# Down-projection of a two-layer hybrid block: the low halves and the sums of squares put on VectorE, the last squares given buffers of their own

## The chip, the core and the metric

The kernel runs on one core of a Trainium2 chip. The metric is the time of one execution on the device in microseconds, the median of several. The engines are called by the profile's names: PE (TensorE, matrix products; PEld is its weight loads), DVE (VectorE), ACT (ScalarE), POOL (GpSimd) and SP (SyncE, which issues most of the transfers). Each works through its own queue in order and waits for the others by semaphores.

## The reference

Two layers work on 1024 latent tokens and 256 context tokens of width 1024, all in float32. What matters here is the end of each layer, a squared-ReLU MLP with a hidden width of 4096, and the norm that follows it:

```python
def rmsnorm(x, g):
    xf = x.astype(jnp.float32)
    y = xf * lax.rsqrt(jnp.mean(xf * xf, axis=-1, keepdims=True) + EPS)
    return (y * g.astype(jnp.float32)).astype(x.dtype)

def sqrelu_mlp(h, w_up, w_down):
    return jnp.square(jax.nn.relu(h @ w_up)) @ w_down
...
        x = x + ga2 * sqrelu_mlp(modulate(rmsnorm(x, g_norm2[l]), sh2, sc2), w_up[l], w_down[l])
        if not last:
            ...
            xc = xc + ga2c * sqrelu_mlp(modulate(rmsnorm(xc, g_norm2[l]), sh2c, sc2c), w_up[l], w_down[l])
    return rmsnorm(x, g_final)
```

The change touches the product with `w_down`, the residual add behind it, and the sum of squares for the next norm.

## The kernel before

Activations lie transposed: features on the 128 partitions, tokens along the row. Block 0 and block 1 are 512 latent tokens each, block 2 is the context (only in layer 0, where the flag `ctx_all` is set). `xT[b]` holds eight tiles of block b's residual stream and `ss[b]` its running sum of squares.

**Products in three passes.** A product must be more exact than one pass of PE. Every operand is therefore split: the high half is a rounded copy made on ACT (L147), the low half is the difference of the operand and that copy (L148), on DVE or POOL. `mm3` then takes high times high (L134), high times low (L135) and low times high (L136).

**Which engine makes a low half** is set by a letter pattern. `lo_(pat)` counts its calls and returns POOL where the pattern has a G and DVE where it has a V. The down-projection's pattern is `DL`, used by `cAt` and `cBt`, which split the two operands of a product into the eight buffers of the tile `A1` (the activations' `cA`, the weights' `cB`; in layer 0 a ninth in a tile `c`). The combinations' pattern `DA` is all V.

**The down-projection** sums over the hidden width in four chunks. A chunk takes a 2 by 2 grid of blocks by Strassen's scheme: seven calls of `run`, each four steps of twelve matmuls, on ready blocks or on sums and differences of blocks that `comb` makes in place (L1445, two instructions of 128x1024 on DVE for each). The blocks lie in `r2`, `A0` and `wr` tiles. In layer 0 each chunk also does the context rows in one pass (`ctx_part`, L1466).

**The residual add** is `put` (L1420, DVE): it multiplies a result in PSUM, or a copy of it in SBUF, by the gate and adds it to `xT[b]`. In the last chunk each `put` of a tile also squares the tile on ACT into a scratch buffer `sc` (L1425) and adds it to `ss[b]` (L1426); the first square of a block goes into `ss[b]` directly (L1423). `psl` is a list of spare half tiles; `sc` is its entries 8 to 11 (two halves of a `c` tile, then `p` or `wf` tiles).

**The norm behind it.** `rstd_bcast` sums `ss[b]` over the partitions by PE (L194), takes the inverse root by three Newton steps of tiny instructions on DVE (L175 to L187) and spreads it over the partitions by PE (L201). After layer 0, `raw` (L1190, L1192) makes the next layer's input of it. After layer 1, `finish_(0)` copies the factor of block 0 into `sc[1]` (L1481), multiplies five tiles by it on POOL (L1487) and three on DVE (L1489), and stores them. Block 1 ends in two halves of 256 tokens: `put`-like adds (L1576), squares (L1577), sums (L1578), two norms, and outputs on POOL (L1587) and DVE (L1590).

**Order.** The program is written as one stream; a scheduler with its own estimates of durations sets each engine's order. A change of engines therefore also moves neighbours.

Of the kernel before, what the change touches and what calls it, by code (L numbers as in the profile page):

```python
# [9 lines left out]
ALU = mybir.AluOpType  # L10
# [24 lines left out]
FA = "V"  # L35
LF = "V"
DA = "V"
DL = "VVVG"
RQ = "MAAV"
NQ = (3, 8)  # L40
GU = 7
SE = ((1, 1), (1, 0))
GL = 100
TQ = 1
LNE = (0, 1)
# [18 lines left out]
def build(tc, A, out, dbg=None):  # L64
# [9 lines left out]
    def T(pool, shape, dt=F32, tag=None, **kw):  # L74
        if tag in alias:
            tag, kw = alias[tag], {}
            if isinstance(tag, tuple):
                pool, tag = tag
        assert kw == seen.setdefault((id(pool), tag), kw) or not kw, tag
        kw = seen[(id(pool), tag)]  # L80
        return pool.tile(list(shape), dt, tag=tag, name=nm(tag), **kw)
# [24 lines left out]
    V, S, G, PE = nc.vector, nc.scalar, nc.gpsimd, nc.tensor  # L106
# [211 lines left out]
    ss = [T(xp, [128, BLK[b][1]], tag=f"ss{b}") for b in range(3)]  # L318
# [109 lines left out]
    for l in range(2):  # L428
        last = l == 1
# [172 lines left out]
        sc = V.tensor_tensor_scan  # L602
# [439 lines left out]
        xT, ss, yT, wo = [None] * 3, [None] * 3, [None] * 3, []  # L1042
# [190 lines left out]
        def csplit(src, pat, c=None):  # L1233
            c = ctile() if c is None else c
            split((c[:, 0], c[:, 1]), src, lo=lo_(pat))
            return c
# [16 lines left out]
        def P_(tag="p"):  # L1253
            return T(*((wk, [128, 512]) if tag == "p" else (ring, [128, 512])), tag=tag)
# [141 lines left out]
        psl = [t[:, i] for t in ct for i in range(2)] + [P_() for _ in range(3 if ctx_all else 9)]  # L1396
        if ctx_all:
            psl += [P_("wf") for _ in range(3)]
        u2, u3, sc = psl[0:4], psl[4:8], psl[8:12]
        nc_ = [0, 0]  # L1400

        def cAt(src):
            nc_[0] += 1
            return csplit(src, DL, cA[nc_[0] % len(cA)])

        def cBt(src):
            nc_[1] += 1
            return csplit(src, DL, cB[nc_[1] % len(cB)])

# [5 lines left out]
        def gains(b, j):  # L1415
            return modT[l][:, BLK[b][2], 40 + j:41 + j]

        def put(b, j, src, sq=None, eng=None):
            xj = xT[b][:, j]
            V.scalar_tensor_tensor(xj, src, gains(b, j), xj, ALU.mult, ALU.add)  # L1420
            if sq is not None:
                if nss[b] == 0:
                    S.activation(ss[b], xj, AF.Square)  # L1423
                else:
                    S.activation(sq, xj, AF.Square)  # L1425
                    (eng or G).tensor_tensor(ss[b], ss[b], sq, ALU.add)  # L1426
                nss[b] += 1

        wdn = A["w_dn"][l].rearrange("(p h) q t -> p h q t", h=2)
        NCH = NPR // 4  # L1430
        E0, E1 = [(G, V)[i] for i in SE[l]]
        blk = {}
# [23 lines left out]
        def ctx_part(c, lastc):  # L1456
            f = A2t[:, c % 2]
            for i in range(2):
                nc.sync.dma_start(f[:, 2 * i:2 * i + 2], dac[4 * c + 2 * i:4 * c + 2 * i + 2].rearrange("p q t -> q p t"))
            ps = banks("Y")  # L1460
            for q in range(2):
                for jj in range(4):
                    o = ps[2 * q + jj // 2][:, 256 * (jj % 2):256 * (jj % 2) + 256]
                    for h in range(2):
                        for k in range(4):
                            PE.matmul(o, blk[f"B{h + 1}{q + 1}"][k][:, 128 * jj:128 * jj + 128], f[:, k, 256 * h:256 * h + 256],  # L1466
                                      start=h + k == 0, stop=h * k == 3)
                    put(2, 4 * q + jj, o, sc[jj][:, :256] if lastc else None)
# [27 lines left out]
        for c in range(NCH):  # L1496
            lastc = c == NCH - 1
# [13 lines left out]
            for j in range(4):  # L1511
                put(0, j, X[j])
# [4 lines left out]
            for j in range(4):  # L1517
                put(0, j, Y[j], sc[j] if lastc else None)
# [38 lines left out]
            for j in range(4):  # L1557
                S.copy(u3[j], X[j])
            for j in range(4):
                put(1, 4 + j, u3[j], sc[j] if lastc else None, E1)  # L1560
            if not lastc:
                p3()
            if lastc and last:
# [5 lines left out]
                for th in range(2):  # L1569
# [4 lines left out]
                    for j in range(4):  # L1574
                        xj, sq = xT[1][:, j, tl], u2[j][:, tl]
# [107 lines left out]
def make(A, dbg=None):  # L1683
    import concourse.bacc as _bacc
    nc = _bacc.Bacc("TRN2", target_bir_lowering=False, num_devices=1)
    aps = {}
    for name, a in A.items():
        aps[name] = nc.dram_tensor(f"in_{name}", a.shape, mybir.dt.from_np(a.dtype), kind="ExternalInput").ap()
    o = nc.dram_tensor("out_0", (128, 8, 1024), F32, kind="ExternalOutput").ap()
    with tile.TileContext(nc, schedule_with_timeline_sim=True) as tc:  # L1690
        build(tc, aps, o, dbg)
    return nc
# [9 lines left out]
```

## Time and profile before

| quantity | value |
|---|---|
| median of 3 runs | 3015.47 us (3014.15 to 3018.77) |
| profiled execution | 3019.14 us, of which the span of the trace is 3017.3 us |
| down-projection of layer 0, with the norm behind it | about 1238 to 1690 us |
| down-projection of layer 1, to the end | about 2661 to 3017 us |
| mean granted clock of PE | 0.962 |

How to read it: the profile names an instruction by line, engine and tiles (output, then inputs, without buffer numbers). A group's row gives its count, its busy time, the mean duration, the idle time of the engine before its members and what ended most of that. A row of the timeline gives the start, the duration, and in brackets the idle time ahead of it and what ended it. The table of stages gives for each stretch the busy time of each engine, then the clock that PE was granted (1.00 is full speed).

### The profile page before, as it was taken

The numbers are of one execution on the slowest core, as the hardware profiler recorded it, in microseconds if no ns is written. First come the engines' busy times: TensorE is split into PE (matmuls) and PEld (weight loads), VectorE is DVE, ScalarE is ACT, GpSimd is POOL, SyncE is SP. The second block draws the span as 40 slices with busy tenths as digits, with TensorE's granted clock in tenths as the row PEclk, the third lists the DMA queues.
The fourth block names the chain that finished last, engine by engine and source line by source line (L and its number), as shares of the span: only waits on it lengthen the run. The fifth ranks groups of instructions, "written<-read, shape, count | busy, mean of one in ns | idle before, by whom it ended". The sixth has DMA issues, their size and how long they took to land.

```text
span 3017.3 us, 40556 instructions
## 1 busy us (share of the span) xinstructions
PE 2827.9 (94%) x14320; PEld 2334.7 (77%) x14320; DVE 2128.6 (71%) x4170; ACT 1178.6 (39%) x2283; POOL 517.3 (17%) x517
## 2 busy tenths in 40 slices
PE   7988989989989999999999898899999999989996
PEld 6877867757878888888887787867767788868885
DVE  8769668742498898786787527468633976678887
ACT  3322245443353333243245432245433534334444
POOL 4213100011200000021125133100022000013334
PEclk7999999999999999999999999899999999999998
DMA  6514575323355544633121212455134443253321
GB/s 237 161 55 128 146 174 156 110 91 120 109 175 175 168 171 165 240 112 116 45 91 56 88 42 85 124 147 147 56 120 139 146 134 115 105 198 99 105 85 56
DMA packets 277871, 376.44 MB, mean 125 GB/s; under 512 B 63396, under 2 KB 154468, under 8 KB 276004
## 3 DMA queue, kind: packets, MB, share of 16 engines
q1 hardware_dynamic: 274788, 366.51, 39.0%
q0 software_dynamic: 576, 4.20, 0.4%
q10 hardware_dynamic: 2304, 3.15, 0.3%
q8 instruction: 113, 1.85, 0.3%
q14 instruction: 90, 0.74, 0.1%
HBM read 283.74 MB, written 90.02 MB: 124 GB/s over the span
## 4 chain that ended last, share of the span: by engine, by line
PE 59%; DVE 18%; DMA 10%; issue 6%; POOL 2%; ACT 2%; SPq 0%; DVEq 0%; POOLq 0%; ACTq 0%
PE mm L138 9%; PE mm L143 7%; PE mm L144 7%; PE v L1141 4%; PE mm L135 4%; PE mm L136 4%; PE mm L134 4%; DVE junk L235 3%; DVE A L148 2%; DVE ac L677 2%; PE mm L1466 2%; PE mm L140 2%; PE mm L141 2%; DMA wf<-in_w_mt 2%; PE t L1466 2%
## 5 line engine op out<-in xcount | busy, mean ns | idle before, releaser
L138 PE MATMUL mm<-A,wr 128*128 128x512 f32 (+1 forms) x840 | 312.9, 375 | 24.6 <-ACT rb L673 12.3
L135 PE MATMUL mm<-A 128*128 128x512 f32 (+1 forms) x654 | 251.3, 389 | 11.2 <-DVE A L148 8.9
L134 PE MATMUL mm<-A 128*128 128x512 f32 (+1 forms) x654 | 238.1, 387 | 5.6 <-ACT A L147 4.4
L136 PE MATMUL mm<-A 128*128 128x512 f32 (+1 forms) x654 | 242.9, 387 | 0.3 <-DVE A L148 0.3
L138 PEld LDWEIGHTS mm<-A,wr 128*128 128x128 f32 x840 | 161.2, 193 | 54.0 <-ACT rb L673 14.0
L143 PE MATMUL mm<-A,wr 128*128 128x512 f32 (+1 forms) x520 | 193.0, 372 | 6.2 <-DVE A L148 4.2
L144 PE MATMUL mm<-A,wr 128*128 128x512 f32 (+1 forms) x520 | 191.6, 369 | 0.0
L1141 PE MATMUL v<-PT,Vt 128*97 128x512 f32 (+1 forms) x336 | 172.8, 599 | 16.6 <-ACT PT L1140 16.1
L138 PE MATMUL mm<-A,c 128*128 128x512 f32 (+1 forms) x520 | 184.0, 355 | 4.5 <-ACT A L147 3.4
L143 PE MATMUL mm<-A,c 128*128 128x512 f32 (+1 forms) x520 | 184.3, 355 | 2.7 <-DVE A L148 2.6
L144 PE MATMUL mm<-A,c 128*128 128x512 f32 (+1 forms) x520 | 182.5, 353 | 1.3 <-DVE c L148 1.3
L148 POOL TENSOR_TENSOR wr<-wf,wr 128x512 fp32r<-128x512 f32 x88 | 123.7, 1413 | 292.1 <-ACT wr L147 230.3
L147 ACT ACTIVATE A<-wr 128x512 fp32r<-128x512 f32 x188 | 114.2, 625 | 147.9 <-PE mm L135 59.2
L147 ACT ACTIVATE A<-A 128x512 fp32r<-128x512 f32 x174 | 106.9, 625 | 160.0 <-PE mm L135 86.6
L148 DVE TENSOR_TENSOR A<-wr,A 128x512 fp32r<-128x512 f32 x146 | 128.7, 893 | 43.4 <-ACT A L147 29.0
L235 DVE SCALAR_TENSOR_TENSOR junk<-wf,t 128x512 bf16<-128x512 f32 x192 | 130.8, 681 | 33.7 <-DMA wf<-in_w_mt 32.0
L135 PEld LDWEIGHTS mm<-A 128*128 128x128 f32 x654 | 123.9, 190 | 39.4 <-DVE A L148 11.7
L1140 ACT ACTIVATE PT<-s 128x512 f32<-128x512 f32 (+1 forms) x168 | 97.0, 583 | 138.6 <-PE s L144 138.0
L134 PEld LDWEIGHTS mm<-A 128*128 128x128 f32 x654 | 123.1, 189 | 31.2 <-ACT A L147 6.8
L136 PEld LDWEIGHTS mm<-A 128*128 128x128 f32 x654 | 123.5, 189 | 25.0 <-DVE A L148 0.7
L138 PE MATMUL mm<-wr,A 128*128 128x256 f32 x464 | 133.4, 288 | 6.6 <-ACT rb L673 4.7
L143 PE MATMUL mm<-wr,A 128*128 128x256 f32 x464 | 133.1, 288 | 0.0
(497 smaller groups left out, 7802.9 us busy)
## 6 DMA issues: line engine op xcount, KB each, us to landing
wf<-in_w_mt SPq DMA_DIRECT2D x96, 256.0 KB
x<-in_w_up SPq DMA_DIRECT2D x40, 512.0 KB
r<-in_w_up SPq DMA_DIRECT2D x38, 512.0 KB
wr<-in_w_dn SPq DMA_DIRECT2D x36, 512.0 KB
gt<-in_w_mt SPq DMA_DIRECT2D x64, 256.0 KB
da<-wf SPq DMA_DIRECT2D x64, 256.0 KB
da<-p SPq DMA_DIRECT2D x64, 256.0 KB
wf<-in_w_in SPq DMA_DIRECT2D x56, 256.0 KB
```

The costliest lines, as they stand in the source:

```text
L134: PE.matmul(ps, lh, rh, start=first, stop=False, skip_group_check=True)
L135: PE.matmul(ps, lh, rl, start=False, stop=False, skip_group_check=True)
L136: PE.matmul(ps, ll, rh, start=False, stop=last, skip_group_check=True)
L138: PE.matmul(ps, lh, rh, start=first, stop=False)
L143: PE.matmul(ps, lh, rl, start=False, stop=False)
L144: PE.matmul(ps, ll, rh, start=False, stop=last)
L147: (hi or S).activation(dst[0], src, AF.Copy) if (hi is None or hi is S) else hi.tensor_copy(dst[0], src)
L148: (lo or G).tensor_tensor(dst[1], src, f32(dst[0]), ALU.subtract)
L235: V.scalar_tensor_tensor(junk, f, 1.0, cb[w], ALU.mult, ALU.mult, accum_out=(ga, modT[l])[kh][:, w, j:j + 1])
L1140: S.activation(PT[:, :nq], ps[:, :nq], AF.Exp, scale=scale)
L1141: PE.matmul(po[:97, :nq], Vt[kt // 2][:, kt % 2, h % 2], PT[:, :nq], start=i == 0, stop=i == len(kts) - 1)
L1466: PE.matmul(o, blk[f"B{h + 1}{q + 1}"][k][:, 128 * jj:128 * jj + 128], f[:, k, 256 * h:256 * h + 256], start=h + k == 0, stop=h * k == 3)
```

## The change

- The pattern `DL` becomes "V": all low halves of the down-projection are made on DVE. One in four was on POOL, 56 in each layer.
- `put` always adds the squares on DVE. On POOL were all of block 0 (7 in each layer), those of block 2 (7 in layer 0) and three of block 1 in layer 1. The argument `eng` (and with it `SE` and `E1`) is no longer read.
- In layer 1 the squares of block 1's tiles 4 to 7 go into `psl[12]` to `psl[15]`, not into `sc`, whose entry 1 holds the factor of block 0 at that time.

```diff
-DL = "VVVG"
+DL = "V"
-SE = ((1, 1), (1, 0))
+SE = ((1, 1), (1, 1))
...
                     S.activation(sq, xj, AF.Square)
-                    (eng or G).tensor_tensor(ss[b], ss[b], sq, ALU.add)
+                    V.tensor_tensor(ss[b], ss[b], sq, ALU.add)
...
             for j in range(4):
-                put(1, 4 + j, u3[j], sc[j] if lastc else None, E1)
+                put(1, 4 + j, u3[j], (psl[12 + j] if last else sc[j]) if lastc else None, E1)
```

In all 136 instructions leave POOL's queue (517 to 381) and join DVE's (3834 to 3970). Three places show how the order changes.

The end of layer 0. POOL's queue before, where `ss0` collects the squares of block 0 among low halves of this stage (`A1`) and of the next stage's weights (`wr_24..`):

```order
L148 TENSOR_TENSOR A1_2293_11789<-wr_2295_11791,A1_2293_11789 128x512
L1426 TENSOR_TENSOR ss0_2319_11815<-ss0_2319_11815,p_2314_11810 128x512
L1426 TENSOR_TENSOR ss0_2319_11815<-ss0_2319_11815,wf_2315_11811 128x512
L148 TENSOR_TENSOR wr_2408_14427<-r2_2305_11801,wr_2408_14427 128x512
L1426 TENSOR_TENSOR ss0_2319_11815<-ss0_2319_11815,wf_2316_11812 128x512
L148 TENSOR_TENSOR A1_2293_11789<-A0_2292_11788,A1_2293_11789 128x512
L1426 TENSOR_TENSOR ss0_2319_11815<-ss0_2319_11815,wf_2317_11813 128x512
```

DVE's queue there in the changed kernel:

```order
L1426 TENSOR_TENSOR ss0_2319_11815<-ss0_2319_11815,p_2314_11810 128x512
L1420 SCALAR_TENSOR_TENSOR x0_2318_11814<-t_2393_14046,mod0_6_66,x0_2318_11814 128x512
L148 TENSOR_TENSOR c_2310_11806<-A0_2292_11788,c_2310_11806 128x512
L148 TENSOR_TENSOR A1_2293_11789<-A0_2292_11788,A1_2293_11789 128x512
L1426 TENSOR_TENSOR ss0_2319_11815<-ss0_2319_11815,wf_2315_11811 128x512
L148 TENSOR_TENSOR A1_2293_11789<-A0_2292_11788,A1_2293_11789 128x512
L148 TENSOR_TENSOR A1_2293_11789<-wr_2300_11796,A1_2293_11789 128x512
L1426 TENSOR_TENSOR ss0_2319_11815<-ss0_2319_11815,wf_2316_11812 128x512
L148 TENSOR_TENSOR A1_2293_11789<-A0_2292_11788,A1_2293_11789 128x512
L1426 TENSOR_TENSOR ss0_2319_11815<-ss0_2319_11815,wf_2317_11813 128x512
```

The sums now stand between DVE's own low halves; of POOL's rows only the weights (`wr_24..`) stay there.

The first chunk of layer 1, where DVE makes the first combinations. A piece of the difference of DVE's queues (`r2`, `wr`, `A0` are operand blocks, `A1` the split ones):

```order
-L1445 TENSOR_TENSOR r2_3871_22709<-wr_3867_22705,r2_3871_22709 128x1024
 L1445 TENSOR_TENSOR A0_3859_22697<-A0_3859_22697,wr_3870_22708 128x1024
-L1445 TENSOR_TENSOR r2_3872_22710<-wr_3868_22706,r2_3872_22710 128x1024
 L148 TENSOR_TENSOR A1_3860_22698<-wr_3870_22708,A1_3860_22698 128x512
+L1445 TENSOR_TENSOR r2_3871_22709<-wr_3867_22705,r2_3871_22709 128x1024
 L1420 SCALAR_TENSOR_TENSOR x0_3887_22725<-mm_3895_22821,mod1_7_67,x0_3887_22725 128x512
 L1420 SCALAR_TENSOR_TENSOR x0_3887_22725<-mm_3896_22822,mod1_7_67,x0_3887_22725 128x512
+L1445 TENSOR_TENSOR r2_3872_22710<-wr_3868_22706,r2_3872_22710 128x1024
```

The two combinations into `r2` move back, behind the combination and the low half of `wr_3870` and, the second, behind two residual adds.

The end of layer 1. POOL's queue before:

```order
L148 TENSOR_TENSOR A1_3860_22698<-wr_3868_22706,A1_3860_22698 128x512
L1487 TENSOR_TENSOR A0_3939_24720<-x0_3887_22725,c_3877_22715 128x512 x5
L1426 TENSOR_TENSOR ss1_3890_22728<-ss1_3890_22728,c_3877_22715 128x512
L1426 TENSOR_TENSOR ss1_3890_22728<-ss1_3890_22728,p_3878_22716 128x512
L1426 TENSOR_TENSOR ss1_3890_22728<-ss1_3890_22728,p_3879_22717 128x512
L1587 TENSOR_TENSOR A0_3939_24720<-x1_3889_22727,c_3875_22713 128x256 x6
```

DVE's queue in the changed kernel, from the last sum of the second half (L1578) on; the three sums of tiles 5 to 7 stand some 25 rows ahead of it:

```order
L1576 SCALAR_TENSOR_TENSOR x1_3889_22727<-mm_3930_24328,mod1_7_67,x1_3889_22727 128x256
L196 TENSOR_SCALAR rb_v_3947_24930<-mm_3946_24927 128x2
L175 TENSOR_SCALAR rs_h_3949_24933<-rb_v_3947_24930 128x2
L1578 TENSOR_TENSOR ss1_3890_22728<-ss1_3890_22728,c_3874_22712 128x256
L176 TENSOR_SCALAR rb_y_3948_24932<-rb_v_3947_24930 128x2
L185 TENSOR_TENSOR rs_t_3950_24936<-rb_y_3948_24932 128x2
L186 TENSOR_TENSOR rs_t_3950_24936<-rs_t_3950_24936,rs_h_3949_24933 128x2
L1489 SCALAR_TENSOR_TENSOR A0_3939_24720<-x0_3887_22725,vec_4_62,c_3877_22715 128x512 x3
L187 SCALAR_TENSOR_TENSOR rb_y_3948_24932<-rs_t_3950_24936,rb_y_3948_24932 128x2
L196 TENSOR_SCALAR rb_v_3952_25012<-mm_3951_25009 128x2
```

The sums leave POOL's queue behind the five L1487. On DVE the three L1489, which before stood ahead of the second half's adds, now stand inside the Newton steps of the first half's norm.

## The prediction

> **What bounds the kernel now.** I read the engines' shares first, then a table of the stages that the change touches, then PE's stalls in them, and last what stands on DVE and POOL ahead of each stall.
>
> ```profile
> PE 2827.9 (94%) x14320; PEld 2334.7 (77%) x14320; DVE 2128.6 (71%) x4170; ACT 1178.6 (39%) x2283; POOL 517.3 (17%) x517
> ...
> core 0: us, PE busy (x) PEld busy (x) DVE busy (x) ACT busy (x) POOL busy (x), PEclk, DMA share, GB/s
> 1230.00:1690.00 460.00, 440.77 (x1960) 369.23 (x1959) 349.92 (x452) 179.77 (x326) 121.51 (x82) 0.98 0.31 105
> 2660.00:2985.00 325.00, 308.51 (x1361) 252.79 (x1360) 278.79 (x355) 156.55 (x279) 119.47 (x63) 0.98 0.30 98
> ...
> 2985.00:3017.30 32.30, 10.57 (x69) 9.72 (x68) 19.38 (x52) 5.43 (x13) 15.68 (x14) 0.63 0.38 131
> ...
> 2770.05:2847.48 77.43, 76.65 (x337) 62.93 (x337) 66.86 (x87) 36.24 (x64) 28.33 (x15) 1.00 0.34 109
> ```
>
> PE is the bound. In one full chunk of layer 1 (the last row) it works 76.65 of 77.43 us at full clock, 76.65 / 337 = 0.227 us a matmul, and the change leaves its 14320 matmuls as they are. So only PE's stalls can be won, and DVE, at 66.86 us in that chunk, must not overtake it. The stalls behind DVE or POOL in the stages touched, with the idle time in brackets:
>
> ```profile
> 1264.54 9.69 PE L1466 MATMUL mm<-A,A 128*128 128x256 f32 x32 [4.30 <-DVE x L1420]
> ...
> 1661.52 1.27 PE L194 MATMUL t<-ones,ss 128*128 128x1 f32 x8 [3.42 <-POOL ss L1426]
> ...
> 2681.81 0.50 PE L135 MATMUL mm<-A 128*128 128x512 f32 x1 [2.19 <-DVE A L148]
> 2691.46 1.19 PE L134 MATMUL mm<-A 128*128 128x512 f32 x4 [3.17 <-ACT A L147]
> 2699.00 0.79 PE L135 MATMUL mm<-A 128*128 128x512 f32 x1 [6.34 <-DVE A L148]
> 2770.05 0.72 PE L135 MATMUL mm<-A 128*128 128x512 f32 x2 [0.78 <-POOL A L148]
> ...
> 2924.86 0.73 PE L135 MATMUL mm<-A 128*128 128x512 f32 x2 [0.78 <-POOL A L148]
> 2955.90 0.47 PE L134 MATMUL mm<-A 128*128 128x512 f32 x1 [1.17 <-DVE x L1420]
> ...
> 3001.54 1.84 PE L194 MATMUL mm<-ones,ss 128*128 128x1 f32 x8 [10.25 <-DVE ss L1578]
> ```
>
> The first two are of layer 0. The stall of 0.78 stands three times in layer 1, once a chunk (first and last shown). The last row is the tail: PE waits 10.25 us for the sums of squares.
>
> **What a moved instruction costs DVE.** First alone, then beside POOL, then the group rows of layer 1 (2660 to 2985 us).
>
> ```profile
> 2964.30 0.69 DVE L148 TENSOR_TENSOR A<-A,A 128x512 fp32r<-128x512 f32 x1
> 2964.90 0.68 DVE L148 TENSOR_TENSOR A<-wr,A 128x512 fp32r<-128x512 f32 x1
> ...
> 2970.91 1.70 DVE L148 TENSOR_TENSOR A<-A,A 128x512 fp32r<-128x512 f32 x1
> ...
> 2974.24 1.78 DVE L148 TENSOR_TENSOR A<-A,A 128x512 fp32r<-128x512 f32 x1
> ...
> 2972.14 3.32 POOL L1426 TENSOR_TENSOR ss<-ss,p 128x512 f32<-128x512 f32 x2
> ...
> L148 DVE TENSOR_TENSOR A<-A,A 128x512 fp32r<-128x512 f32 x75 | 62.3, 842 | 12.6 <-ACT A L147 11.0 <-PE mm L134 1.6
> L148 DVE TENSOR_TENSOR A<-wr,A 128x512 fp32r<-128x512 f32 x77 | 56.8, 752 | 24.0 <-ACT A L147 9.5 <-PE mm L135 8.1 <-PE t L135 4.8
> L1420 DVE SCALAR_TENSOR_TENSOR x<-mm,mod,x 128x512 f32<-128x512 f32 x52 | 36.9, 738 | 0.0
> L1420 DVE SCALAR_TENSOR_TENSOR x<-c,mod,x 128x512 f32<-128x512 f32 x32 | 26.6, 873 | 1.3 <-ACT c L1531 1.3
> ...
> 2752.89 1.23 DVE L1445 TENSOR_TENSOR r<-wr,r 128x1024 f32<-128x1024 f32 x1 [1.20 <-POOL A L148]
> ```
>
> Alone, low halves follow each other every 0.60 us (2964.90 less 2964.30). While POOL works on its sums (2972.14) the same instruction takes 1.70 to 1.78, so each POOL instruction beside DVE costs DVE about 1.1 us. The change adds 63 instructions to DVE in this stage (56 low halves, 7 sums), POOL's x63 of the table: 63 x 0.60 = +37.8 us. What it relieves, against 0.683 alone: 75 x 0.159 = 11.9, 77 x 0.069 = 5.3, and for the adds from SBUF, against the 0.737 of those from PSUM, 32 x 0.136 = 4.4; together 21.6 us, or 0.34 per POOL instruction, since many of these ran beside a DVE that was idle or read PSUM. DVE also no longer waits for POOL (1.20 in the last row). Per full chunk: 14 low halves, +8.4, less 14 x 0.34 = 4.8, less two such waits, 2.4: about +1. DVE then holds some 68 to 70 of 77.4 us, below PE's 76.65, so the cost is hidden by PE as long as the order lets it. If that cover goes, the bill is the +8.4 unrelieved.
>
> [...]
>
> **Layer 0, body (a): 0.** DVE is busy 349.92 of 460 us; 70 more instructions x 0.60 = 42 fit under PE's 440.77. A low half that waits for ACT now stands on DVE's queue in the first chunk, with adds queued behind it, some of which feed the stall at 1264.54. I take 0, the DVE being idle a quarter of the time; bounds are one contended step either way, -1.1 to +1.1.
>
> **Layer 0, end (b): -3.5.**
>
> ```profile
> 1659.77 1.70 POOL L1426 TENSOR_TENSOR ss<-ss,wf 128x512 f32<-128x512 f32 x1
> ...
> 1664.08 0.63 PE L134 MATMUL mm<-A 128*128 128x512 f32 x1
> 1664.51 0.63 PE L135 MATMUL mm<-A 128*128 128x512 f32 x1
> ...
> 1661.50:1666.00 4.50, 4.48 (x17) 3.81 (x18) 4.50 (x9) 2.28 (x5) 1.64 (x1) 0.62 0.00 0
> ```
>
> L194 waits for the last sum, which POOL ends at 1661.47. In the changed order I walked DVE from 1634.2: 22 low halves and 4 sums x 0.60, 5 adds x 0.66, a small one of 0.35, and the six of the next stage's weights that POOL keeps x 1.1 give 25.9 us, so the sum is done by about 1660.1 at the latest, and without four of the six contentions (DVE reads PSUM or is ahead) at 1655.7. PE has been idle since 1658.10. A little behind the middle I take 1658.7, where PE keeps 0.6 of its 3.42 us: -2.8. Behind the stall PE's matmuls come every 0.43 us in place of 0.227, granted clock 0.62, for about six matmuls: 1.3 us, of which I take half back, -0.7. Bounds: all of it, 3.42 + 1.3 = -4.7, and nothing, if the sums stand as late as now.
>
> [...]
>
> **Layer 1, first chunk (c): -1.8.** DVE is saturated here and PE waits for it.
>
> ```profile
> 2665.08 2.32 DVE L1445 TENSOR_TENSOR A<-wr,A 128x1024 f32<-128x1024 f32 x1
> 2669.67 2.38 DVE L148 TENSOR_TENSOR A<-A,A 128x512 fp32r<-128x512 f32 x2
> 2674.84 1.77 DVE L148 TENSOR_TENSOR A<-A,A 128x512 fp32r<-128x512 f32 x1
> ```
>
> Six low halves come from POOL: +3.6. The rows give back 2.32 - 1.23, 2.38 - 1.29 and 1.77 - 0.69, 3.3 us, and the other three POOL instructions about 0.37 each, 4.4 in all. Walked by the new order, PE resumes at 2680.1 for 2681.81 and at 2697.2 for 2699.00. Bounds: -4 if all relief and no cost lies ahead of the stalls, +1 if the combinations moved back are met by PE.
>
> **Layer 1, body (d): -2.0.**
>
> ```profile
> 2764.56 7.14 POOL L148 TENSOR_TENSOR A<-wr,A 128x512 fp32r<-128x512 f32 x2 [7.45 <-ACT A L147]
> ```
>
> The stall at 2770.05 waits for POOL, whose two low halves take 7.14 us there against 0.60 each on DVE. Three such and the 1.17 make 3.5. Late next is DVE's own row, margins under 0.5 us by my walk, so I take 2.0; bounds -3.5 and, if each chunk waits 0.5 more, +1.5.
>
> **Tail (e): -2.7.**
>
> ```profile
> 2986.53 5.32 DVE L1489 SCALAR_TENSOR_TENSOR A<-x,vec,c 128x512 f32<-128x512 f32 x3 [0.64 <-ACT c L1481]
> ...
> 2986.56 7.68 POOL L1487 TENSOR_TENSOR A<-x,c 128x512 f32<-128x512 f32 x5 [7.72 <-ACT c L1481]
> 2996.32 2.60 POOL L1426 TENSOR_TENSOR ss<-ss,p 128x512 f32<-128x512 f32 x2
> 2998.95 2.77 DVE L1578 TENSOR_TENSOR ss<-ss,c 128x256 f32<-128x256 f32 x8 [5.54 <-POOL ss L1426]
> ...
> 3004.06 0.16 DVE L187 SCALAR_TENSOR_TENSOR rb_y<-rs_t,rb_y 128x2 f32<-128x2 f32 x1
> ...
> 3004.87 1.22 PE L201 MATMUL mm<-cst,rb_y 128*128 128x128 f32 x4 [1.50 <-DVE rb_y L187]
> 3007.36 0.65 DVE L187 SCALAR_TENSOR_TENSOR rb_y<-rs_t,rb_y 128x2 f32<-128x2 f32 x1
> ```
>
> Now POOL's sums come behind its five L1487 and end at 2998.92; L1578 and PE follow, and after L194 the norm, outputs and stores take 3017.3 - 3001.54 = 15.8 us. With the sums on DVE and in buffers of their own, they no longer wait for the products that read `sc[1]`: done near 2992.5, 6.4 us earlier. But the three L1489 leave their place ahead and stand in the first half's Newton steps: 2993.0 + 5.3 = 2998.3, beside POOL to about 3000.7. Of the eight tiny steps behind, two are blocked (1.3 each, a POOL instruction's length), six at about 0.19 (3004.06's 0.16 and the gap to the next): the norm's factor at about 3002, against 3004.87 before, where L201 takes it up, -2.8; 0.1 off for the halves, which end closer together, -2.7. Bounds: unblocked, 2998.3 + 8 x 0.2 = 2999.9, -5; each step at the 0.65 of 3007.36, -1.4 or worse, -0.1. No moved instruction issues a transfer; SP's queue changes only in that one store of block 0 stands behind one of block 1, not the last one, 0.
>
> **Sum:** -3.5 - 1.8 - 2.0 - 2.7 = -10.0 us. The profiled execution took 3019.14 us, span 3017.3 and 1.84 around it, which is 3.67 above the median; the span becomes 3007.3, that execution 3009.1, the median 3005.5.
>
> **Rivals.**
> - *Same.* The order gives back what the relief brings: c and d at 0, the sums of b end only 1 us sooner because they stand behind more low halves, the tail at its -1.4: 3013.1. For it: my walks leave margins under 0.5 us. Against it: the relief in the first chunk is in the rows.
> - *Slower.* DVE becomes the bound in layer 1. If only half of the relief and of the waits comes (3.6 of 7.2 per chunk), a chunk adds 8.4 - 3.6 = 4.8, some 14 us in three, less b and e: 3015.5 + 14.4 - 6.2 = 3023.7. It decides when what a chunk adds ahead of a product exceeds the lead of one step, 12 x 0.227 = 2.7 us. For it: 68 to 70 of 77 us leaves little room in an order fixed by estimates. Against it: the contended rows of 1.7 us vanish for certain.
> - *Better.* PE keeps its clock at b (-4.7), the tail is unblocked (-5), c and d at -4 and -3.5: -17.2, 2998.3. With a at -1.1 too, 2997.2.
>
> **How the numbers follow.** 0.2% is 6 us, about what a measurement of this kernel can tell from no change. Forecast (3001 to 3009.4) 0.47; better 0.13, so faster 0.60; same 0.26; slower 0.14. The range leaves about a tenth out at each side: 2996, just below the better case, and 3018, which holds the same case and the lesser half of what lies between it and the slower one. The forecast's own range is 3001 to 3010.
>
> **What would show it.** b: L194 at the end of layer 0 idles under 1 us and the clock stays near 1.00. c: the stalls at 2681 and 2699 shorter by 1 to 2 us. d: no 0.78 behind POOL, a chunk's PE near 76.7 of 76.9 us, DVE 67 to 70, low halves at 685 ns throughout the chunks. e: L1578 without its 5.54 us, the three L1489 between L186 and L187, and L201 near 3002 less the 7.3 us won before. Wrong would be PE idle behind DVE low halves once a chunk (slower), or the first Newton behind L1489 far past 3002 (e at nothing).

## The result and the profile after

The changed kernel took 3001.61 us (median of 5, 2995.2 to 3008.1) against 3015.47 us: a ratio of 0.995, 95% interval 0.9932 to 0.9969, 13.9 us less. A gain of ten was forecast, 3005.5 in a range of 2996 to 3018. The profiled execution has a span of 2996.5 us, 20.8 less than the profiled one before.

First PE's stalls of the changed kernel, those that answer to the rows shown of before:

```profile
1260.48 8.86 PE L1466 MATMUL mm<-A,A 128*128 128x256 f32 x32 [3.82 <-DVE x L1420]
...
1652.32 1.05 PE L194 MATMUL t<-ones,ss 128*128 128x1 f32 x8 [0.42 <-DVE ss L1426]
...
2672.43 0.50 PE L135 MATMUL mm<-A 128*128 128x512 f32 x1 [1.84 <-DVE A L148]
2679.44 2.08 PE L134 MATMUL mm<-A 128*128 128x512 f32 x4 [4.89 <-ACT A L147]
2684.89 0.80 PE L135 MATMUL mm<-A 128*128 128x512 f32 x1 [3.37 <-DVE A L148]
...
2763.01 0.50 PE L135 MATMUL mm<-A 128*128 128x512 f32 x1 [0.23 <-DVE A L148]
...
2916.46 0.50 PE L135 MATMUL mm<-A 128*128 128x512 f32 x1 [0.23 <-DVE A L148]
2938.62 0.47 PE L134 MATMUL mm<-A 128*128 128x512 f32 x1 [1.01 <-ACT A L147]
...
2983.76 1.22 PE L201 MATMUL mm<-cst,rb_y 128*128 128x128 f32 x4 [8.48 <-DVE rb_y L187]
```

The 3.42 us at the end of layer 0 are 0.42. The three stalls of 0.78 behind POOL are 0.23 behind DVE. In the tail PE no longer waits 10.25 us for the sums; it waits 8.48 us for the factor behind them. Two stretches of the same kernel, a full chunk of layer 1 and the 4.5 us behind L194 (columns as in the first fence of the prediction), and DVE's groups in layer 1:

```profile
2763.01:2839.73 76.72, 76.48 (x336) 62.93 (x337) 71.08 (x101) 35.93 (x65) 0.00 (x0) 1.00 0.33 110
...
1652.30:1656.80 4.50, 4.48 (x24) 3.88 (x25) 4.50 (x10) 2.04 (x4) 0.00 (x0) 1.00 0.14 58
```

```profile
L148 DVE TENSOR_TENSOR A<-wr,A 128x512 fp32r<-128x512 f32 x100 | 66.8, 686 | 17.8 <-ACT A L147 17.8
L148 DVE TENSOR_TENSOR A<-A,A 128x512 fp32r<-128x512 f32 x92 | 62.1, 686 | 8.7 <-ACT A L147 8.7
L1420 DVE SCALAR_TENSOR_TENSOR x<-c,mod,x 128x512 f32<-128x512 f32 x32 | 22.6, 747 | 0.0
```

A chunk lasts 76.72 us for 77.43, PE works all but 0.24 of it, and DVE is busy 71.08. The low halves take 686 ns where they took 842 and 752, the adds from SBUF 747 for 873. Behind L194 the granted clock is 1.00 where it was 0.62.

**Where the time went.** I cut each profiled execution at six places on PE: the first product of the context rows (L1466, behind its stall), the transpose behind the 4.03 us stall near 1628, the first L138 behind the stall of 6.5 to 6.9 near 1678, the first matmul of layer 1's down-projection, its third stall (2684.89 above), and the stall near 2940 us. The stretches are called a, b, mid, c, d, e; they add up to the span.

| kernel | to the 1st place | a | b | mid | c | d | e |
|---|---|---|---|---|---|---|---|
| before | 1264.54 | 366.48 | 51.96 | 979.11 | 36.91 | 256.90 | 61.40 |
| changed | 1260.48 | 365.08 | 46.60 | 978.18 | 34.55 | 253.73 | 57.88 |
| changed, again | 1266.71 | 364.87 | 46.63 | 979.78 | 34.55 | 254.15 | 58.01 |
| low halves alone | 1263.31 | 364.99 | 46.84 | 983.23 | 34.55 | 255.42 | 61.06 |
| sums, own buffers | 1262.27 | 364.96 | 50.66 | 973.27 | 36.91 | 256.40 | 58.23 |
| no own buffers | 1265.40 | 366.47 | 46.67 | 981.42 | 34.55 | 254.13 | 59.16 |
| POOL work, layer 1 | 1260.69 | 365.09 | 46.60 | 980.59 | 40.89 | 270.64 | 58.00 |
| POOL work, layer 0 | 1258.89 | 365.35 | 46.61 | 976.84 | 34.54 | 253.69 | 58.18 |
| DVE's products late | 1263.88 | 365.06 | 46.62 | 977.44 | 34.55 | 253.77 | 58.98 |
| all on DVE | 1263.46 | 365.09 | 46.61 | 978.11 | 34.55 | 253.83 | 55.65 |
| all on DVE, late | 1265.65 | 365.06 | 46.65 | 977.98 | 34.55 | 254.14 | 56.27 |
| another tail | 1263.84 | 365.05 | 46.59 | 981.32 | 34.54 | 253.70 | 55.66 |

The change is worth -1.4 (a), -5.4 (b), -2.4 (c), -3.2 (d) and -3.5 (e), together -15.8 us; the rest of the 20.8, 4.1 and 0.9, lies in the first column and in mid. Those two hold most of the scatter. The stretches a and d hold a little: each starts behind a stall, where PE's granted clock is low at first (0.51 in the first 3.1 us of d in the changed kernel, 0.50 in the first 4.0 before) and for a time that differs between executions of one program: the first 40 matmuls of d take 10.6 us in one profile of the changed kernel and 11.0 in the other. Without their first 40 matmuls the change is worth -0.6 in a (355.22 to 354.65 us) and -2.6 in d (245.72 to 243.13), and its second profile repeats both within 0.02; the sum is then -14.4.

### The profile page after: what moved, and what is told of

The parts are those of the page before. It is cut to its first block, busy times and chain, and to the rows that moved or that the text cites. A ratio compares the mean times of both kernels' runs of the same rounds, so it can differ in the third digit from the quotient of the medians.

```text
span 2996.5 us, 40427 instructions
## 1 busy us (share of the span) xinstructions
PE 2822.4 (94%) x14320; PEld 2332.5 (78%) x14320; DVE 2134.6 (71%) x4306; ACT 1177.7 (39%) x2283; POOL 290.1 (10%) x381
## 4 chain that ended last, share of the span: by engine, by line
PE 60%; DVE 20%; DMA 11%; issue 4%; ACT 2%; POOL 1%; SPq 0%; DVEq 0%; POOLq 0%; ACTq 0%
PE mm L138 8%; PE mm L143 6%; PE mm L144 6%; PE mm L135 5%; PE mm L134 5%; PE mm L136 5%; PE v L1141 4%; DVE junk L235 3%; DMA wf<-in_w_mt 3%; DVE ac L677 2%; PE mm L1466 2%; PE t L1466 2%; PE mm L140 2%; PE mm L141 2%; DVE A L148 2%
## 5 line engine op out<-in xcount | busy, mean ns | idle before, releaser
L138 PE MATMUL mm<-A,wr 128*128 128x512 f32 (+1 forms) x840 | 315.7, 379 | 19.0 <-DVE x L1420 6.9
L135 PE MATMUL mm<-A 128*128 128x512 f32 (+1 forms) x654 | 249.7, 386 | 5.9 <-DVE A L148 5.9
L136 PE MATMUL mm<-A 128*128 128x512 f32 (+1 forms) x654 | 247.2, 386 | 0.0
L134 PE MATMUL mm<-A 128*128 128x512 f32 (+1 forms) x654 | 227.8, 387 | 8.1 <-ACT A L147 8.1
L138 PEld LDWEIGHTS mm<-A,wr 128*128 128x128 f32 x840 | 163.4, 196 | 48.0 <-ACT rb L673 7.8
L143 PE MATMUL mm<-A,wr 128*128 128x512 f32 (+1 forms) x520 | 196.4, 378 | 3.8 <-DVE A L148 1.6
L144 PE MATMUL mm<-A,wr 128*128 128x512 f32 (+1 forms) x520 | 194.6, 375 | 0.0
L138 PE MATMUL mm<-A,c 128*128 128x512 f32 (+1 forms) x520 | 183.8, 354 | 6.0 <-ACT A L147 4.4
L138 PE MATMUL mm<-wr,A 128*128 128x256 f32 x464 | 133.8, 289 | 7.3 <-ACT rb L673 4.3
L148 DVE TENSOR_TENSOR A<-A,A 128x512 fp32r<-128x512 f32 x174 | 119.7, 698 | 26.3 <-ACT A L147 23.7
```

The lines of the kernel that those rows point to most:

```text
L134: PE.matmul(ps, lh, rh, start=first, stop=False, skip_group_check=True)
L135: PE.matmul(ps, lh, rl, start=False, stop=False, skip_group_check=True)
L136: PE.matmul(ps, ll, rh, start=False, stop=last, skip_group_check=True)
L138: PE.matmul(ps, lh, rh, start=first, stop=False)
L143: PE.matmul(ps, lh, rl, start=False, stop=False)
L144: PE.matmul(ps, ll, rh, start=False, stop=last)
```

## The experiments

Each ratio below is to the kernel before, run again beside the experiment; its median was 3015.47 to 3020.33 us in these series, so medians of two experiments can't be compared directly.

**Does the scatter belong to the change?** The changed kernel once more.

> The changed kernel once more, beside the kernels of this call, to see which spans repeat. Theory: the stretches that the change touches repeat within 0.3 us (from the first matmul of layer 1's down-projection to the third stall 34.55, from there to the stall near 2938 us 253.7, from there to the end 57.9), while the time until the first product of layer 0's down-projection and the stretch between the layers, whose instructions the change leaves alone, differ by up to 5 us from run to run, which is the scatter of the whole. Rival: the 4.8 us that the changed kernel was ahead before its first changed instruction belong to it and come again.

Median 2999.07 us, ratio 0.9943 (0.9929 to 0.9957). One row of its PE:

```profile
1266.71 8.64 PE L1466 MATMUL mm<-A,A 128*128 128x256 f32 x32 [4.00 <-DVE x L1420]
```

It reached the first place 6.2 us later than the first time (1260.48), later even than the kernel before, and its b, c, d and e came again within 0.42 us. So the rival falls: the lead before the first changed instruction was chance. Over the twelve profiles the first column runs from 1258.89 to 1266.71 and mid from 973.27 to 983.23. A single execution can't tell effects under about 10 us; the stretches can.

**The parts alone.** The low halves alone:

```diff
-DL = "VVVG"
+DL = "V"
```

> The change's first part alone: the pattern DL becomes V, so the 112 low halves leave POOL; the sums of squares stay on POOL, as before, and in the old buffers. Theory, the gain is a sum of places: POOL's queue at the end of layer 0 loses the low halves that stood among its sums, so the stall before L194 shrinks from 3.42 to 1.5 us or less and its half-clock matmuls go (b -3 to -5); the first chunk of layer 1 gains 2.4 and the three 0.78 stalls shrink to about 0.2 with DVE's low halves at 685 ns (d about -3); the tail keeps its 10.25 us before L194, since POOL's three sums still stand behind the five L1487 (e 0 within 0.5). In all -9 to -11, about 3005. Rival, what counts is the number of instructions that leave POOL (contention): 112 of 136, so -11.5 spread over all stages, the tail's own share included (-3).

Ratio 0.9965 (0.9952 to 0.9978).

```profile
1655.20 1.05 PE L194 MATMUL t<-ones,ss 128*128 128x1 f32 x8 [0.51 <-POOL ss L1426]
...
2935.41 0.50 PE L135 MATMUL mm<-A 128*128 128x512 f32 x1 [1.15 <-DVE A L148]
...
2993.57 1.84 PE L194 MATMUL mm<-ones,ss 128*128 128x1 f32 x8 [9.94 <-DVE ss L1578]
```

By the stretches -1.5, -5.1, -2.4, -1.5 and -0.3: -10.8. The sums still run on POOL, and yet the stall at the end of layer 0 is 0.51: what made POOL's sums late was the low halves in its queue (a sum itself takes POOL 1.68 us here and 1.70 to 1.83 before). In d a new stall of 1.15 took back part (a chunk is as short as in the change). The tail is untouched, 9.94 for 10.25, against the rival's -3.

The sums on DVE and the own buffers, with the pattern "VVVG":

```diff
-                    (eng or G).tensor_tensor(ss[b], ss[b], sq, ALU.add)
+                    V.tensor_tensor(ss[b], ss[b], sq, ALU.add)
...
-                put(1, 4 + j, u3[j], sc[j] if lastc else None, E1)
+                put(1, 4 + j, u3[j], (psl[12 + j] if last else sc[j]) if lastc else None, E1)
```

> The other two parts alone: all sums of squares on DVE, the last squares in buffers of their own, but one low half in four still on POOL. Theory of places: c and d get nothing (the stalls of 0.78 stay, c within 0.5), the end of layer 0 gets part (DVE's sums now stand among low halves slowed to 1.7 us by POOL: stall 1 to 3 us in place of 3.42, b 0 to -3), the tail its -3 to -5 whole, since the order puts the three L1489 once more in the first half's norm: -4 to -7 in all, about 3010. Rival by number of instructions: 24 of 136, -2.5, about 3013.

Ratio 0.9958 (0.9944 to 0.9971).

```profile
1656.21 1.05 PE L194 MATMUL t<-ones,ss 128*128 128x1 f32 x8 [2.09 <-DVE ss L1426]
...
1658.62 0.63 PE L135 MATMUL mm<-A 128*128 128x512 f32 x1
1659.04 0.63 PE L136 MATMUL mm<-A 128*128 128x512 f32 x1
...
2688.07 0.80 PE L135 MATMUL mm<-A 128*128 128x512 f32 x1 [6.34 <-DVE A L148]
...
2759.09 0.73 PE L135 MATMUL mm<-A 128*128 128x512 f32 x2 [0.77 <-POOL A L148]
...
2988.47 1.01 PE L194 MATMUL mm<-ones,ss 128*128 128x1 f32 x4 [7.68 <-DVE ss L1578]
```

By the stretches -1.5, -1.3, 0, -0.5 and -3.2, together -6.5, as the theory of places had it; the rival's -2.5 falls. In b the stall is 1.3 shorter, and that is all: behind it matmuls again come 0.42 us apart, and from L194 to the end of b it is 21.68 us, no less than the 21.46 before. The timed difference, 12.7 (8.8 to 16.9 by the interval), is larger and lies beyond the -4 to -7 expected. The profiled execution was the lowest of its five and has the shortest mid of all, which is scatter: PE, DVE, ACT and POOL go through the changed kernel's rows there in the same order. But that doesn't explain a median of five; where the 6 us beyond the stretches come from stays open. The change without the own buffers:

```diff
-                put(1, 4 + j, u3[j], (psl[12 + j] if last else sc[j]) if lastc else None, E1)
+                put(1, 4 + j, u3[j], sc[j] if lastc else None, E1)
```

> The change without its third part: low halves and sums on DVE, but the squares of block 1's tiles 5 to 7 go into the old buffers, one of which holds block 0's factor until POOL's five and DVE's three products have read it. Theory of places: b, c, d as in the whole change; in the tail the squares come late as before (POOL's last L1487 ends them), but the sums then take 0.6 us each on DVE where POOL took 1.3, and the L1489 stand ahead of the second half's adds: about 2 us better than before where the whole change was 3.6 better, so the whole change plus 1.5, about 3003. Rival, the buffers are what frees the tail at all: the tail as before, the change plus 3.6, about 3005; second rival, the buffers do nothing: 3001.6.

Ratio 0.9940 (0.9925 to 0.9954), no different from the change. The stretch e shows what the time can't: 59.16, that is 2.2 us better than before and 1.2 short of the mean of the change's two (57.95).

```profile
2991.95 1.86 PE L194 MATMUL mm<-ones,ss 128*128 128x1 f32 x8 [8.01 <-DVE ss L1578]
```

**Contention, or POOL's lateness?** POOL gets work that nothing reads, in the changed kernel:

```diff
+        def ballast(src):
+            if last and sum(nc_) % 4 == 0:
+                G.tensor_tensor(psl[18], src, src, ALU.subtract)
...
         def cAt(src):
             nc_[0] += 1
+            ballast(src)
```

(the same line in `cBt`.)

> The whole change, with POOL given work again in layer 1: at every fourth call that splits an operand in the last down-projection POOL subtracts the same source from itself into a spare tile that nothing reads (37 groups, 54 instructions of 128x512). Nothing waits for POOL, so what it costs is contention alone. Theory: contention at the rate of the kernel before, 0.34 us per POOL instruction, or 4.8 us a chunk, brings DVE from 71.1 to about 76 of 76.7 us a chunk; it becomes as full as PE, and layer 1 loses 2 to 8 us against the change, 3004 to 3010. DVE's low halves rise from 686 to 750 ns or more. Rival, what the change won in layer 1 was POOL's lateness (low halves of 3.6 us that PE waited for), and contention is hidden: DVE slower but layer 1 within 1 us of the change, 3001 to 3003.

Ratio 1.0007 (0.9998 to 1.0016): the whole gain is gone. The stretch c and a chunk, DVE's and POOL's groups, and two stalls:

```profile
2652.97:2693.86 40.89, 24.46 (x100) 19.02 (x100) 40.89 (x45) 13.56 (x24) 20.52 (x11) 0.84 0.42 155
2772.33:2855.01 82.68, 79.05 (x337) 64.36 (x337) 78.76 (x101) 35.91 (x64) 22.22 (x15) 0.96 0.31 102
```

```profile
L148 DVE TENSOR_TENSOR A<-wr,A 128x512 fp32r<-128x512 f32 x92 | 67.6, 753 | 11.2 <-ACT A L147 11.2
...
L1404 POOL TENSOR_TENSOR p<-wr 128x512 f32<-128x512 f32 x27 | 46.7, 1731 | 74.9 <-DVE wr L1451 61.7 <-DMA wr<-in_w_dn 11.6
```

```profile
2688.42 2.07 PE L134 MATMUL mm<-A 128*128 128x512 f32 x4 [10.81 <-ACT A L147]
...
2772.33 0.50 PE L135 MATMUL mm<-A 128*128 128x512 f32 x1 [1.80 <-DVE A L148]
...
2773.47 0.63 PE L135 MATMUL t<-A 128*128 128x512 f32 x1
2773.89 0.63 PE L136 MATMUL t<-A 128*128 128x512 f32 x1
```

The low halves take 753 ns for 686. A chunk's DVE rose from 71.08 to 78.76 us, 7.7 for the 14 POOL instructions that start in it, 0.55 each, and c and d grew by 6.3 and 16.9: 23.2 us where the theory said 2 to 8. The direction is the theory's, the rival falls, the size was missed. A changed order isn't the reason: in c and d PE, DVE and ACT go through the changed kernel's rows in the same order. Nor does DVE wait for POOL: in these stretches its idle time ends on ACT alone. In c DVE works without a pause in both kernels (34.55 us, then 40.89), so the price of 11 POOL instructions, 0.58 each, is the whole of the 6.3. In d 7.1 of the 16.9 us is PE itself, busy 259.14 us for 252.01 with the same 1100 matmuls: behind the stall of 1.80 at 2772.33 they come 0.42 us apart, and the chunk's granted clock is 0.96. The other 9.8 are waits. So it isn't DVE's average that counts. My reading, not tested by itself: POOL's work starts when a combination is ready, and that is just where DVE's next low halves are awaited. The same in layer 0, in its first three chunks (`not last`, `sum(nc_) < 168`, into `psl[11]`):

> The same extra POOL work as in layer 1, now in the first three chunks of layer 0's down-projection: at every fourth call that splits an operand POOL subtracts the source from itself into a scratch tile that nothing reads there (42 instructions of 128x512). Theory (contention costs time only where DVE has no slack): DVE is busy some 76% of this stretch with the change, so 42 x 0.55 us (the extra DVE time per POOL instruction measured in layer 1) = 23 us of DVE time fit under PE, and a chunk stays at 103.8 us within 0.5 (from the product of the context rows in one chunk to that in the next). Rival, each POOL instruction costs its share anyway, as in layer 1: 0.4 us each, 6 us a chunk, 110 us.

Ratio 0.9944 (0.9925 to 0.9963). A chunk's stretch (from the context rows of the second to those of the third) in the changed kernel, then in this one:

```profile
1366.00:1470.00 104.00, 104.00 (x467) 87.52 (x466) 75.76 (x109) 36.54 (x64) 0.00 (x0) 1.00 0.29 92
```

```profile
1366.00:1470.00 104.00, 104.00 (x465) 87.25 (x464) 84.37 (x109) 36.53 (x64) 19.23 (x14) 1.00 0.28 91
```

DVE pays 8.6 us for 14 POOL instructions, 0.61 each, and PE still works every one of the 104 us; the stretch a is 0.27 us longer (365.35 for 365.08), or 0.5 without its first 40 matmuls. The same price is all but hidden where DVE is busy 73% and costs time where it is busy 93%.

**The tail.** What the changed kernel does there, DVE's rows and POOL's:

```profile
2975.18 5.19 DVE L1489 SCALAR_TENSOR_TENSOR A<-x,vec,c 128x512 f32<-128x512 f32 x3
2980.29 1.21 DVE L187 SCALAR_TENSOR_TENSOR rb_y<-rs_t,rb_y 128x2 f32<-128x2 f32 x1
...
2981.54 1.18 DVE L185 TENSOR_TENSOR rs_t<-rb_y 128x2 f32<-128x2 f32 x1
2982.76 0.16 DVE L186 TENSOR_TENSOR rs_t<-rs_t,rs_h 128x2 f32<-128x2 f32 x1
...
2975.22 7.49 POOL L1487 TENSOR_TENSOR A<-x,c 128x512 f32<-128x512 f32 x5 [648.13 <-ACT c L1481]
```

The three products take 5.19 beside POOL, two steps of the norm behind them 1.2 each, and from POOL's end at 2982.71 on a step takes 0.16. First, block 0's products are issued behind the second half's last Newton step:

```diff
+                products()
                 for th in range(2):
...
+                with behind("rs"):
                     if k in PK0:
                         G.tensor_tensor(o, xT[0][:, k], sc[1], ALU.mult)
```

> The change, with block 0's eight final products (five on POOL, three on DVE) held back behind the Newton steps of both halves of block 1. In the changed kernel PE idles 8.48 us before the first half's factor: 5.2 in the three L1489 and twice 1.2 in Newton steps that stand beside POOL. Theory (a tiny step with two operands in SBUF waits a whole POOL instruction): with DVE and POOL both clear, the eight steps take 0.2 us each, the first factor is there near 1.8 us after the sums and the second soon after, 5 to 7 us sooner; the outputs then queue up, DVE's three contended products and ten scalings and POOL's eleven, and the end comes 2 to 4 us sooner. Rival: the end is set by the stores, 4 MB that now all start late, and comes at the same time or up to 3 us later.

Ratio 0.9960 (0.9948 to 0.9973).

```profile
2978.09 1.11 DVE L185 TENSOR_TENSOR rs_t<-rb_y 128x2 f32<-128x2 f32 x1
...
2982.89 1.19 DVE L186 TENSOR_TENSOR rs_t<-rs_t,rs_h 128x2 f32<-128x2 f32 x1
2984.11 0.16 DVE L187 SCALAR_TENSOR_TENSOR rb_y<-rs_t,rb_y 128x2 f32<-128x2 f32 x1
...
2977.92 6.14 POOL L1490 TENSOR_TENSOR A<-x,c 128x512 f32<-128x512 f32 x5 [648.29 <-ACT c L1481]
```

That the expectation missed: the order holds within one engine's queue, and POOL's queue held nothing to stand behind, so its five products started at once, at 2977.92. The kernel became a clean measurement instead: beside five POOL instructions of 1.23 us each exactly five tiny steps took 1.11 to 1.19 us (first and last shown), the sixth 0.16. The end came 1.1 us later than in the change (58.98). Then POOL out of it, `PK0 = ()`, all eight products on DVE in the old place (the profile is that of its second run):

> The change, with all eight final products of block 0 on DVE and none on POOL, in the same place. Theory of contention: eight alone take 8 x 0.66 = 5.3 us, as long as the three beside POOL took (5.19), and the Newton steps behind them run at 0.2: PE's 8.48 us before the first factor becomes about 7.0, the second factor comes 2.5 us sooner, the end 2 to 2.5 sooner, and POOL saves five instructions. Rival (no contention, each engine at its own speed): eight times 1.73 = 13.8 us, the end 6 to 8 us later.

> The kernel with block 0's eight final products all on DVE, in their place in the first half's norm, once more, since its profile fell into a disturbed execution. Theory as before, with the eight-product price measured since (6.82 us for eight, beside POOL's three): the products take 5.4 to 6.8 us, the steps behind them 0.2 each, PE idles about 7 to 8.3 us before the first factor (8.5 in the changed kernel), the end from 0.3 to 2 us sooner.

Ratios 0.9936 (0.9923 to 0.9948) and 0.9949 (0.9930 to 0.9968).

```profile
2978.18 5.39 DVE L1489 SCALAR_TENSOR_TENSOR A<-x,vec,c 128x512 f32<-128x512 f32 x8
...
2983.67 0.16 DVE L185 TENSOR_TENSOR rs_t<-rb_y 128x2 f32<-128x2 f32 x1
```

Eight products alone take 5.39 us, three beside POOL's five took 5.19. The steps run at 0.16, and e is 55.65, 2.2 us less than in the change. All eight on DVE and late as well:

> Both together: all eight products on DVE, and held back behind both halves' Newton steps. Theory: the first factor 5 to 7 us sooner as with everything held back, the second near 3 us sooner than that of the products in the old place; then DVE has eight products and nine scalings in a row, 9 us, in part beside POOL's six, and ends within 1 us of the changed kernel's: the end 0 to 2 us sooner, less than with the products in the old place. Rival: the factors are all that counts, the end 4 us or more sooner.

Ratio 0.9940 (0.9926 to 0.9953).

```profile
2981.97 0.71 PE L201 MATMUL mm<-cst,rb_y 128*128 128x128 f32 x4 [1.30 <-DVE rb_y L187]
```

PE's wait for the first factor falls from 8.48 to 1.30 us, and the end comes only 1.6 us sooner (56.27): the factor is no longer what sets it. Last, five products on DVE that read the factor in PSUM, and three on POOL behind its six of block 1:

> The change with another tail: block 0's products stand behind both halves' Newton steps, five on DVE that read the factor in PSUM, and three on POOL behind POOL's six products of block 1, so that no POOL instruction runs beside the Newton steps of the first half. Theory: the first factor 38 us after the stall near 2938 us and the second 42.3, as in the kernel with all eight late (37.94 and 42.30); DVE's ten scalings and five products read one operand from PSUM and don't contend (0.41 and 0.74 each), so that DVE ends near 50.2 and POOL near 50 after that stall, in place of 53.7 in the changed kernel: the end 2 to 4 us sooner than the change's 57.9. Rival, the end is set by 3 MB of stores that start late: 56.3, as in the kernel with all eight late, or later.

Median 2995.85 us, ratio 0.9928 (0.9908 to 0.9947), the lowest of all, though its interval overlaps the change's.

```profile
2992.07 2.04 DVE L1599 SCALAR_TENSOR_TENSOR A<-x,vec,mm 128x256 f32<-128x256 f32 x5
...
2991.12 3.81 POOL L1495 TENSOR_TENSOR A<-x,c 128x512 f32<-128x512 f32 x3
```

Here five DVE scalings with an operand in PSUM run beside POOL at 0.41 each, as the four of the changed kernel's 1.65 us at 2988.47 do without POOL, and POOL at 1.27 each: neither pays. DVE and POOL end about 49 to 50 us after the stall near 2945, as expected, but e is 55.66, as with the simple `PK0 = ()`: behind POOL's last product 5.8 us pass until the end, in the change 4.1 (2992.42 to 2996.5). The rival has that part: the stores that start late give back what the engines win. The 16 DMA engines are busy 0.87 of the last 11.6 us here, and 0.62 of the change's last 11.5.

## Why the prediction was right, and where it was off

The forecast was -10.0 and -13.9 was measured, with 15.8 in the touched stretches of the profile, of which 1.4 lies in the first 40 matmuls of a and d, chance at least in part; each of the four terms had its sign and was too small.

- *a, forecast 0, -1.4.* Of this 0.8 lies behind the stall at the first place, and is chance: the first 40 matmuls take 11.25 us before (granted clock 0.50 in the first 3.5) and 10.2 to 10.4 in most others (0.60 in the changed kernel's first 3.6), but 11.79 in the kernel without own buffers, whose layer 0 is that of the change. The other 0.6 comes later and is there with either part alone and without own buffers; half of it is a stall of 0.28 near 1601 that is gone.
- *b, forecast -3.5, -5.4.* The stall fell from 3.42 to 0.42, as walked (0.6). The step that failed is the clock: "of which I take half back, -0.7". From L194 to the end of b it was 21.46 us before (1661.52 to 1682.98) and is 19.84, 1.6 less: the whole of it. The granted clock was 0.62 behind the 3.42 us and is 1.00 behind the 0.42; that half of the price would come back was an estimate that no row of before had set. In two other runs it fell behind shorter stalls: matmuls came 0.42 us apart behind the 2.09 us of the sums alone and the 1.80 of POOL's extra work. They stayed 0.23 apart behind stalls up to 1.63, but also in the seven behind the changed kernel's 1.84 at 2672.43; and at a wait for POOL near 1815, in instructions that both kernels share, the clock was 1.00 behind 2.25 us (before, 1820.14) and 0.54 behind 2.30 (changed, 1810.40). So these runs set no length from which it falls. Another 0.7 was won ahead of L194, which I hadn't priced.
- *c, forecast -1.8, -2.4.* DVE is the bound, as said, and its relief is in the groups above: the three stalls shrink from 11.70 us in all to 10.10, and PE's own work from 25.21 to 24.45. The walk didn't hold: in the new order the first stall comes twelve matmuls later and is 0.35 shorter, not 1 to 2, the second is 1.7 longer, the third 3.0 shorter.
- *d, forecast -2.0, -3.2.* A chunk is 0.71 shorter, three make 2.1, and the last stall gives 0.2; I kept margins of half a microsecond against DVE that DVE didn't need. Another 0.6 lies in the first 40 matmuls behind the third stall, 11.2 us before and 10.6 here, and is chance in part: in the second profile d is 0.4 longer.
- *DVE's load, forecast 68 to 70 us a chunk, 71.08.* 14 low halves add 8.4 and 4.2 came back, where I had 4.8 and two waits, which aren't busy time. The cover held, but the rival "slower" was close: 14 foreign POOL instructions a chunk were enough to lose the whole gain. A tiny step took nearly a whole POOL instruction, 1.11 to 1.19 us beside five of 1.23, and 0.16 without. The mean over a chunk of layer 1 is less, 0.55 us for each POOL instruction of 1.7.
- *e, forecast -2.7, -3.5.* Right in mechanism to the step: the three L1489 stand in the norm, two steps behind them are slow. No run shows a step of the forecast's 1.3 us, the length of a POOL instruction: beside POOL's five of 1.50 the two took 1.21 and 1.18, and the longest in the tail before was 0.65. DVE reached them 0.5 us sooner than walked, and 0.3 of the gain was lost behind the last factor.

## What to carry to other kernels

Where both worked here, a POOL instruction of 128x512 cost DVE 0.55 to 0.61 us as a mean over a chunk, and a tiny step in a chain ran 1.11 to 1.21 us beside POOL for 0.16, while DVE's scalings with an operand in PSUM kept their 0.41. Leave such work on POOL where DVE has slack (73% busy here), and take it out where DVE is nearly full (93% here) or runs a serial chain. A stall can cost PE more than its length: behind the 3.42 us at the end of layer 0 matmuls came 0.43 us apart for 0.23 at a granted clock of 0.62. An engine's queue makes work late that it could finish in time, as the low halves did to POOL's sums (a stall of 3.42 us with them in the queue, 0.51 without). To judge a change of a few tenths of a per cent, compare the stretches between fixed instructions, not whole executions, and leave out the first matmuls behind a stall at which the clock fell (40 of them took 10.2 to 11.8 us here).

## What the runs showed that I had not expected

Eight products on DVE alone (5.39 us) cost DVE as much as three beside POOL's five (5.19 to 5.25): sharing such work out gained nothing. Behind stalls of 1.80 and 2.09 us PE's matmuls came 0.42 us apart, as they did behind 3.42. And the same program reached the same instruction up to 6.2 us earlier or later (1260.48 and 1266.71).
